# A decoder layer on one core: q and k rotated in fewer operations, one more pair of `up` and two more tiles of the last `dn` group by seven half products

## The chip, the cores and the metric

The kernel runs on one core of a Trainium2 chip. The core has five engines with a queue of instructions each: TensorE (PE in the profile; its weight loads are shown apart as PEld), VectorE (DVE), ScalarE (ACT), GpSimd (POOL), which here only sets memory and issues accumulating DMAs, and SyncE (SP), which issues loads and stores. They meet through semaphores. Times are device microseconds of one execution; the metric is the median of several executions.

## The reference

One decoder layer over 512 tokens of width 1024, in fp32. Cut to what matters:

```python
h = rms_norm(x, mix_norm_g)
u, q, kv, nsa_g, merge_g = split(h @ w_in)
y_pool = pooling_mixer(u, pool_w, pool_scale) @ w_pool_out
y_nsa  = nsa_mixer(q, kv..., gates) @ w_nsa_out      # q, k: rms_norm, then partial_rope; three branches
x = x + (gate_pool * y_pool + gate_nsa * y_nsa) @ w_out
h = rms_norm(x, ffn_norm_g)
gate_pre, val = split(h @ w_up)                      # 2 x 2816 columns
x = x + (silu(causal_dwconv(gate_pre, conv_w, conv_b)) * val) @ w_down

def partial_rope(x, pos):                            # the first 16 of 64 columns of a head
    x1, x2 = x[..., :8], x[..., 8:16]
    return concat([x1 * cos - x2 * sin, x2 * cos + x1 * sin, x[..., 16:]])
```

## The kernel before

**Arithmetic.** Matrices are multiplied in a reduced form of fp32, with each operand split into a high and a low part. A product of one 128x128 block of weights is then three matmuls: high by high, high by low, low by high. The splits are made by ScalarE (the high part is a rounding copy) and VectorE (the low part is a subtraction), or, in `split_by_dma`, by ScalarE and an accumulating DMA that POOL issues, with no VectorE work.

**Stages.** `first` and `round_a` project q and two of the k slots for all tokens, in PSUM banks held over eight rounds. A second group of projections gives the values and gates. Then two streams of PE work run side by side: "m", the attention (rotation, transposes, scores, softmax, averages), and "f", the projections of pooling and merge gates. Then come the output projections (`wno`, `wout`), then the gated MLP: 22 pairs `f` of a gate tile and a value tile of `w_up`, and `w_down` in four groups `dn` of four pairs each, whose work is put between the pairs as `fill`, and a last group `dz` over the pairs 16 to 21, which also adds the residual and stores the result.

**Rotation.** For each of the four tiles of 128 tokens, `rotate(t)` weights and rotates the 16 leading columns of 8 q heads and 4 k heads. The q tile is first multiplied by its norm weights (`gq`); then `rope_on` makes two half products with the sine (one for each half), one with the cosine and one sum. All of it is VectorE work on the tiles `qp`, `kp` and `rt`. The result is transposed by PE (`qk_transpose`). The tables `rope` are computed earlier.

**A pair in plain form** (`up_plain`): the weights of 128 output columns come in one load of 512 KB per half, and 24 matmuls of 512 token columns make the gate, 24 the value.

**A pair in half products** (`up_fast`): gate and value tile are taken as a 2x2 block problem (two halves of the depth, two halves of the tokens) and computed with seven products of half size in place of eight, each of 12 matmuls of 256 columns. For this `half_weights` forms sums of weight quarters on VectorE (`s3`, `r1`, `rg`), and splits seven weight operands: two of them as one tile of 1,024 columns, one of 512 by ScalarE and VectorE (`sh`, `sl`), four of 512 by accumulating DMA. The moving operands (`th`, `tl`) are sums of halves of x, made once in `sums`. Two of the seven products of a pair (`end1`, `end2`) are held and issued in the next pair. Before, pairs 0 and 2 are plain (`PLAIN`), all others in half products.

**The last group** has eight tiles. `dz_plain` makes a tile with 18 matmuls of 512 columns; `dz_fast` makes two tiles with seven half products of 9 matmuls of 256. Their moving operands are `yh`, `yl` and the sums `yth`, `ytl`, made in `y_sums` from y of two pairs three apart. Before, tiles 0 and 1 are plain, and 2 to 7 go in three calls of `dz_fast`.

**What sets the order.** All calls go to a planner (`Plan`), which records them with their dependences and prices and, with a list scheduler, makes one fixed order for each engine. PE's order inside a stream is that of the program; the two streams of the first part are interleaved by the planner, and the other engines' orders are its choice by due times. Tiles come from pools (54 pages of 128x512, rings of three for the raw, high and low weights), and a step whose tile isn't free waits. In `half_weights` the loads of the second weights (`r1`, `r2`) wait for an earlier product, named through the list `begun`.

Of the kernel before, what the change touches and what calls it, by code (L numbers as in the profile page):

```python
# [15 lines left out]
P = 128  # L16
T = 512
NT = 4
# [3 lines left out]
DH = 64  # L22
# [27 lines left out]
NCST = _o  # L50
PAGES = 54
RINGS = {"wraw": 3, "whi": 3, "wlo": 3}
PLAIN = (0,2)
DIRECT = (0,)
AT = (5, 9, 13, 17)
FILL = {f: (0, 0, 0, 0) for f in range(22)}
# [341 lines left out]
def hybrid_layer(ctx: ExitStack, tc: tile.TileContext, xT, xa, pos, par, cst, poolw, w1, wa, wb, wf,  # L398
# [3 lines left out]
    PE, ACT, DVE, POOL, SP = pl.engines  # L402
# [8 lines left out]
    def page(name, shape=(P, T), dt=F32):  # L411
        return pl.tile(sb, shape, dt, name, "pg", PAGES)
# [6 lines left out]
    def keep(name, shape, dt=F32, bufs=1):  # L419
        return pl.tile(sb, shape, dt, name, "t_" + name, bufs)  # L420
# [174 lines left out]
    rope = keep("rope", (P, 2, 5, 2, 8))  # L595
    gq = keep("gq", (P, DH))[:, 0:16]
# [22 lines left out]
    DVE.tensor_copy(rope[:, 0, :, 1], rope[:, 0, :, 0])  # L619
    DVE.tensor_scalar_mul(rope[:, 1, :, 0], rope[:, 1, :, 1], -1.0)  # L620
    DVE.tensor_scalar_mul(gq, ng[:, 0, 0:16], -0.125)
    DVE.tensor_copy(gkv[:, :, 0:16], ng[:, 1:4, 0:16])
    DVE.scalar_tensor_tensor(gkv[:, :, 16:DH], ng[:, 0:1, 16:DH].to_broadcast([P, 3, DH - 16]), -0.125, ng[:, 1:4, 16:DH], op0=ALU.mult, op1=ALU.mult)

# [45 lines left out]
    DVE.tensor_mul(vg, gates[:, :, 0::3].rearrange("p t h -> p h t"),  # L670
                   C("valid")[:, None, :].to_broadcast([P, H, NT]))

    def rope_on(x, tmp, idx, n):
        np_ = x.shape[0]
        ct = rope[:np_, 0, idx].rearrange("p a b -> p (a b)")
        for o, i in ((0, 1), (1, 0)):
            DVE.tensor_mul(tmp[:, :, o * 8:(o + 1) * 8], x[:, :, i * 8:(i + 1) * 8],
                           rope[:np_, 1, idx, o][:, None, :].to_broadcast([np_, n, 8]))
        DVE.tensor_mul(x[:, :, 0:16], x[:, :, 0:16], ct[:, None, :].to_broadcast([np_, n, 16]))
        DVE.tensor_add(x[:, :, 0:16], x[:, :, 0:16], tmp)  # L680

    def rotate(t):
        x, y = qp[t], kp[t]
        DVE.tensor_mul(x[:, :, 0:16], x[:, :, 0:16], gq[:, None, :].to_broadcast([P, 8, 16]))
        y4 = y.rearrange("p (b g) d -> p b g d", b=2)
        DVE.tensor_mul(y4, y4, gkv[:, 1:3][:, :, None, :].to_broadcast([P, 2, 2, DH]))
        tmp = page("rt", (P, 12, 16))
        rope_on(x, tmp[:, 0:8], t, 8)
        rope_on(y, tmp[:, 8:12], t, 4)

    for t in range(NT):
        x, y = qp[t], kp[t]
# [12 lines left out]
    def qk_transpose(t):  # L705
# [7 lines left out]
        if t % 2:  # L713
# [6 lines left out]
            for g in range(2):  # L720
# [4 lines left out]
                ACT.activation(y[r], f32(x[o]), AF.Copy)  # L725

    rotate(0)
    rotate(1)
    turned, flipped = [], []
    for t in range(NT):  # L730
        qk_transpose(t)
        turned.append(pl.last())
        if t + 2 < NT:
            with pl.behind(turned[t]):
                rotate(t + 2)
# [137 lines left out]
    x = keep("kcx", (64, 1, DH))  # L873
# [5 lines left out]
    DVE.tensor_scalar(sm[:, 1:2], sm[:, 0:1], 1.0 / DH, EPS, op0=ALU.mult, op1=ALU.add)  # L879
    rsqrt(sm[:, 2:3], sm[:, 1:2], sm[:, 3:4])  # L880
    DVE.scalar_tensor_tensor(x[:, 0], x[:, 0], sm[:, 2:3], gkv[0:64, 0], op0=ALU.mult, op1=ALU.mult)
    rope_on(x, keep("kct", (64, 1, 24))[:, :, :16], 4, 1)
    ks = keep("kcsp", (64, 2, 2, DH), F32R)
    kx = x.to_broadcast([64, 2, DH])
    split(ks[:, 0], ks[:, 1], kx)
# [5 lines left out]
    ct = keep("cst", (P, 3, T), F32R)  # L891
# [184 lines left out]
    turn = [0]  # L1076
# [6 lines left out]
    for c in range(4):  # L1083
        wh, wl = weights(wno[c].rearrange("p a k n -> p (a k n)"), 1024, "v")
        for f in (2 * c, 2 * c + 1):
            o = (f % 2) * 512
# [104 lines left out]
    def up_plain(f):  # L1191
        pts = []
        for s in range(2):
            wh, wl = weights(flat(wup[f, s]), 1024, "v" if f in DIRECT else "d")
            pt = any_bank()
            if f == 0 and s == 1:
                mm3(pt, wh, wl, gh, gl, 0, 5, nk=KD)
                bcast_rstd(rstd2, rb, "tr")
            mm3(pt, wh, wl, gh, gl, 5 if f == 0 and s == 1 else 0, KD)
            pts.append(pt)  # L1200
            if s == 0:
                begun.append(pl.last())
            if f == 0 and s == 0:
                norm_rstd(acc, rstd2, bank("sc", (P, 2, T))[:, 0])
        pg, pv = pts
        y, g = page("y"), page("fg")
        DVE.tensor_mul(g, pg, rb)
        t = conv(f, g, g)
        DVE.tensor_mul(y, pv, rb)
        DVE.tensor_mul(y, y, t)  # L1210
        split_y(f, y)
# [28 lines left out]
    def fill(n, free=False):  # L1240
        for _ in range(n):
            if fills:
                fills.pop(0)(free)
# [100 lines left out]
    for f in range(KF):  # L1344
        if f in AT:
            dn_group(AT.index(f))
        fill(FILL[f][0], True)
        if f in PLAIN:
            up_plain(f)
# [12 lines left out]
    def dz_plain(f):  # L1362
        wh, wl = weights(flat(wdz[f]), 768, "v")
        pt = any_bank()
        o = page("o")
        mm3(pt, wh, wl, yh, yl, 16, KF, koff=16, nk=KF, first=16)
        begun.append(pl.last())
        DVE.tensor_add(o, pt, x2[f])
        SP.dma_start(out[f], o)
# [3 lines left out]
    def dz_fast(f, e):  # L1373
        L, Rr = slice(0, H2), slice(H2, T)
        a11, a12, h1, h2, h3, h4, h5 = half_weights(flat(wdz[f]), (flat(wdz[e, :, 0:3]), flat(wdz[e, :, 3:6])), 384,
                                                    DZ, begun[-4])
        bx, by, bq = any_bank(), any_bank(), any_bank()
        of, oe = page("o"), page("o")
        product(bx, a11, ymov(0, 0), True, 3)
        begun.append(pl.last())  # L1380
        ACT.activation(by[:, L], bx[:, L], AF.Copy)
        product(bq, h1, ymov(2, 0), True, 3)
        DVE.tensor_sub(oe[:, Rr], x2[e][:, Rr], bq[:, L])
        product(by, h2, ymov(2, 1), False, 3)
        DVE.tensor_add(of[:, Rr], by[:, L], x2[f][:, Rr])
        product(bx, a12, ymov(1, 0), False, 3)
        DVE.tensor_add(of[:, L], bx[:, L], x2[f][:, L])
        SP.dma_start(out[f, :, L], of[:, L])
        product(by, h3, ymov(3, 0), False, 3)
        DVE.tensor_sub(oe[:, Rr], oe[:, Rr], by[:, L])  # L1390
        SP.dma_start(out[e, :, Rr], oe[:, Rr])
        product(bq, h4, ymov(1, 1), False, 3)
        DVE.tensor_add(of[:, Rr], of[:, Rr], bq[:, L])
        SP.dma_start(out[f, :, Rr], of[:, Rr])
        product(by, h5, ymov(3, 1), False, 3)
        DVE.tensor_sub(oe[:, L], x2[e][:, L], by[:, L])
        SP.dma_start(out[e, :, L], oe[:, L])

    for f in range(2):
        dz_plain(f)  # L1400
    for f in range(2, 8, 2):
        dz_fast(f, f + 1)

    pl.emit(TRIES, RESERVE)
# [94 lines left out]
```

## Time and profile before

| | us |
|---|---|
| median of 3 runs | 688.55 (687.68 to 693.29) |
| profiled execution | 687.27 |
| its span, first to last instruction | 685.5 |
| TensorE busy in the span | 680.7 (99%) |
| VectorE busy | 518.8 (76%) |
| ScalarE busy | 443.4 (65%) |

The clock granted to TensorE was 1.00. Matmuls are pipelined and their ends are modelled, so a busy TensorE says only that matmuls follow each other; how fast is read from their starts. All operations are recorded by one helper, so every row has its line, L394, and groups are told apart by tiles: `out<-in` names what an operation writes and reads, without buffer numbers. In a row of groups stand the count, then busy us, mean ns of one, and the idle time of the engine just before, with what ended it. PSUM banks are named `mm`, `tr`, `av` and `sc`.

### The profile page before, as it was taken

To read this page: it belongs to the slowest core of one execution; us is meant where nothing else is said; L and a number is where in the kernel's file an instruction comes from. 1 tells how busy PE (TensorE), PEld (TensorE's weight loads), DVE (VectorE), ACT (ScalarE), POOL (GpSimd) and SP (SyncE) were. 2 spreads that over 40 slices of the span, in tenths; PEclk is the share of its full clock that TensorE was granted. 3 is DMA by queue.
4 is the path that set the end of the run, shared out by engine and by line. 5 is a ranking of instruction groups with operands and counts; after the bars stand their busy time and mean duration, and the time that the engine had idled before them with its cause. 6 is when DMAs were issued, how large, how long until landed. Compare 5 with 4: busy or idle time off the path is not lost.

```text
span 685.5 us, 11622 instructions
## 1 busy us (share of the span) xinstructions
PE 680.7 (99%) x4187; PEld 607.8 (89%) x4187; DVE 518.8 (76%) x1138; ACT 443.4 (65%) x811; POOL 108.0 (16%) x135
## 2 busy tenths in 40 slices
PE   9999999999999999999999999999999999999998
PEld 8898888888888888888888999999999999999898
DVE  6768788888887744777777887777778877688984
ACT  7666477776776654346678876565667657567552
POOL 0010210111111110000122232222223122222121
PEclk9999999999999999999999999999999999999999
DMA  8576644535645557745778989687758766866454
GB/s 303 175 185 203 166 100 116 140 89 145 166 116 151 146 142 239 281 139 172 204 162 197 238 181 217 161 191 172 180 127 205 180 155 168 186 150 154 116 135 106
DMA packets 48585, 115.80 MB, mean 169 GB/s; under 512 B 5520, under 2 KB 9360, under 8 KB 48528
## 3 DMA queue, kind: packets, MB, share of 16 engines
q1 hardware_dynamic: 30960, 76.44, 34.0%
q0 software_dynamic: 17424, 38.48, 31.6%
q8 instruction: 33, 0.54, 0.3%
q14 instruction: 24, 0.20, 0.1%
q10 hardware_dynamic: 144, 0.14, 0.1%
HBM read 70.28 MB, written 6.29 MB: 112 GB/s over the span
## 4 chain that ended last, share of the span: by engine, by line
PE 97%; DMA 1%; DVE 1%; ACT 0%; issue 0%; POOL 0%; POOLq 0%
PE mm L394 37%; PE tr L394 34%; PE sc L394 14%; PE av L394 12%; DMA w<-w 1%; ACT kt L394 0%; DVE qp L394 0%; DVE qt L394 0%; ACT wlo L394 0%; DVE u L394 0%; DVE kt L394 0%; DVE o L394 0%; DVE rt L394 0%; POOL ones L394 0%; POOLq L1490 0%
## 5 line engine op out<-in xcount | busy, mean ns | idle before, releaser
L394 ACT ACTIVATE whi<-wraw 128x1024 fp32r<-128x1024 f32 (+2 forms) x91 | 92.7, 1019 | 41.8 <-PE mm L394 16.1
L394 DVE TENSOR_TENSOR wlo<-wraw,whi 128x1024 fp32r<-128x1024 f32 (+1 forms) x63 | 73.3, 1165 | 5.8 <-ACT whi L394 4.1
L394 PE MATMUL mm<-xh,whi 128*128 128x512 f32 x176 | 72.4, 412 | 0.1
L394 PE MATMUL tr<-tl,sh 128*128 128x256 f32 x250 | 70.1, 280 | 0.0
L394 PE MATMUL mm<-xh,wlo 128*128 128x512 f32 x176 | 69.0, 392 | 0.0
L394 PE MATMUL mm<-xl,whi 128*128 128x512 f32 x176 | 68.9, 391 | 0.0
L394 PE MATMUL tr<-th,sl 128*128 128x256 f32 x240 | 67.7, 282 | 0.0
L394 PE MATMUL tr<-th,sh 128*128 128x256 f32 x240 | 67.7, 282 | 0.0
L394 POOL DMA_DIRECT2D sl<-r x43 | 37.1, 862 | 161.9 <-ACT sl L394 90.8
L394 POOL DMA_DIRECT2D wlo<-wraw x28 | 24.3, 868 | 238.4 <-ACT wlo L394 204.9
L394 PE MATMUL mm<-gh,whi 128*128 128x256 f32 (+1 forms) x320 | 60.8, 287 | 0.0
L394 PEld LDWEIGHTS mm<-gh,whi 128*128 128x128 f32 x320 | 49.5, 188 | 0.6
L394 PEld LDWEIGHTS tr<-tl,sh 128*128 128x128 f32 x250 | 47.2, 189 | 0.5
L394 PEld LDWEIGHTS tr<-th,sh 128*128 128x128 f32 x240 | 45.1, 188 | 1.1
L394 PE MATMUL mm<-gh,wlo 128*128 128x256 f32 (+1 forms) x160 | 45.9, 287 | 0.0
L394 PEld LDWEIGHTS tr<-th,sl 128*128 128x128 f32 x240 | 45.1, 188 | 0.0
L394 DVE SCALAR_TENSOR_TENSOR ft<-fg,pr,ft 128x511 f32<-128x511 f32 (+1 forms) x44 | 32.9, 749 | 12.9 <-ACT ft L394 12.2
L394 PE MATMUL sc<-yh,whi 128*128 128x512 f32 x108 | 42.2, 390 | 0.0
L394 PE MATMUL sc<-yl,whi 128*128 128x512 f32 x108 | 42.0, 389 | 0.0
L394 PE MATMUL sc<-yh,wlo 128*128 128x512 f32 x108 | 42.0, 389 | 0.0
L394 ACT ACTIVATE wlo<-wraw 128x1024 fp32r<-128x1024 f32 x28 | 29.7, 1060 | 15.9 <-PE mm L394 12.9
L394 PEld LDWEIGHTS mm<-xh,wlo 128*128 128x128 f32 x176 | 33.0, 188 | 7.4
(422 smaller groups left out, 1994.1 us busy)
## 6 DMA issues: line engine op xcount, KB each, us to landing
wlo<-wraw POOLq DMA_DIRECT2D x28, 512.0 KB, 4.5
wraw<-wup SPq DMA_DIRECT2D x24, 512.0 KB, 4.2
wraw<-wf SPq DMA_DIRECT2D x22, 512.0 KB, 3.5
r<-wup SPq DMA_DIRECT2D x40, 256.0 KB, 4.3
sl<-r POOLq DMA_DIRECT2D x40, 256.0 KB, 5.0
wraw<-wdn SPq DMA_DIRECT2D x16, 512.0 KB, 3.6
sl<-s POOLq DMA_DIRECT2D x20, 256.0 KB, 5.3
sl<-wraw POOLq DMA_DIRECT2D x20, 256.0 KB, 4.3
```

Of the source, the lines that this page charges most:

```text
L394: getattr(self.real[o.eng], method)(*a, **kw)
```

## The change

The sine and cosine tables for q are multiplied once by the norm weights (`ropeq`, three operations), so that a q tile needs no weighting of its own. The two half products with the sine become one, which reads the halves in turned order through a backward step. A rotation of q is then three operations, a rotation of k three and its weighting. Pair 2 of `up` leaves `PLAIN`, and all eight tiles of the last group go by `dz_fast`. The list `begun` gets one entry for each pair of tiles, so the loads of the last group wait for other products than before. The planner makes its order anew for the whole program.

```diff
-PLAIN = (0,2)
+PLAIN = (0,)
...
+    ropeq = keep("ropeq", (P, 2, NT, 2, 8))
+    gq2 = gq.rearrange("p (a b) -> p a b", a=2)
+    DVE.tensor_mul(ropeq[:, 0], rope[:, 0, 0:NT], gq2[:, None].to_broadcast([P, NT, 2, 8]))
+    for o in range(2):
+        DVE.tensor_mul(ropeq[:, 1, :, o], rope[:, 1, 0:NT, o], gq2[:, None, 1 - o].to_broadcast([P, NT, 8]))
...
-    def rope_on(x, tmp, idx, n):
+    def rope_on(x, tmp, table, n):
         np_ = x.shape[0]
-        ct = rope[:np_, 0, idx].rearrange("p a b -> p (a b)")
-        for o, i in ((0, 1), (1, 0)):
-            DVE.tensor_mul(tmp[:, :, o * 8:(o + 1) * 8], x[:, :, i * 8:(i + 1) * 8],
-                           rope[:np_, 1, idx, o][:, None, :].to_broadcast([np_, n, 8]))
-        DVE.tensor_mul(x[:, :, 0:16], x[:, :, 0:16], ct[:, None, :].to_broadcast([np_, n, 16]))
-        DVE.tensor_add(x[:, :, 0:16], x[:, :, 0:16], tmp)
+        cos, sin = (table[i][:np_, None].to_broadcast([np_, n, 2, 8]) for i in range(2))
+        turn = bass.AP(tensor=x.tensor, offset=x.offset + 8, ap=[list(x.ap[0]), [DH, n], [-8, 2], [1, 8]])
+        x4, tmp4 = (q[:, :, 0:16].rearrange("p n (a b) -> p n a b", a=2) for q in (x, tmp))
+        DVE.tensor_mul(tmp4, turn, sin)
+        DVE.tensor_mul(x4, x4, cos)
+        DVE.tensor_add(x[:, :, 0:16], x[:, :, 0:16], tmp[:, :, 0:16])

     def rotate(t):
         x, y = qp[t], kp[t]
-        DVE.tensor_mul(x[:, :, 0:16], x[:, :, 0:16], gq[:, None, :].to_broadcast([P, 8, 16]))
         y4 = y.rearrange("p (b g) d -> p b g d", b=2)
         DVE.tensor_mul(y4, y4, gkv[:, 1:3][:, :, None, :].to_broadcast([P, 2, 2, DH]))
         tmp = page("rt", (P, 12, 16))
-        rope_on(x, tmp[:, 0:8], t, 8)
-        rope_on(y, tmp[:, 8:12], t, 4)
+        rope_on(x, tmp[:, 0:8], [ropeq[:, i, t] for i in range(2)], 8)
+        rope_on(y, tmp[:, 8:12], [rope[:, i, t] for i in range(2)], 4)
...
-    rope_on(x, keep("kct", (64, 1, 24))[:, :, :16], 4, 1)
+    rope_on(x, keep("kct", (64, 1, 24))[:, :, :16], [rope[:, i, 4] for i in range(2)], 1)
...
-    for f in range(2):
+    for f in range(0):
         dz_plain(f)
-    for f in range(2, 8, 2):
+    for f in range(0, 8, 2):
         dz_fast(f, f + 1)
```

## The prediction

> **What bounds the kernel now.** I read the page's busy times first, then the chain that ended last.
>
> ```profile
> PE 680.7 (99%) x4187; PEld 607.8 (89%) x4187; DVE 518.8 (76%) x1138; ACT 443.4 (65%) x811; POOL 108.0 (16%) x135
> ...
> PE 97%; DMA 1%; DVE 1%; ACT 0%; issue 0%; POOL 0%; POOLq 0%
> ```
>
> PE is busy 99% of the span and is 97% of the chain. A busy PE can still be a slow one, so the next question is whether it waits. The view of waits, PE alone, has two rows:
>
> ```profile
> PE mm L394 <- POOL ones L394: 1.0, 1, 1.0
> PE tr L394 <- DVE qp L394: 0.6, 1, 0.6
> ```
>
> So beyond the start this view has one wait of PE, for VectorE's rotated q. Time can go only by giving PE less to do, or by that one wait. What a matmul costs is read from the chain in order of time (start, us, what, count), where PE runs without a break:
>
> ```profile
> 337.04 5.44 PE tr L394 x24
> ...
> 367.76 5.44 PE av L394 x24
> ...
> 373.20 1.42 PE mm L394 x12
> ...
> 655.97 4.08 PE mm L394 x18
> ...
> 669.63 3.19 PE tr L394 x27
> ```
>
> The first row is the last tile of `wout`: 24 matmuls of 512 columns take 5.44 us, 0.227 each, and a half product of 12 matmuls of 256 columns takes 1.42, 0.118 each: half the columns cost 52% of the time, not 50%. The row at 367.76 is the value half of pair 2 itself, the row at 655.97 is tile 1 of the last group (18 matmuls), and the row at 669.63 is three half products of tiles that already run in the new form (9 matmuls, 1.063 each).
>
> What the other engines have left is read by stage (PE, PEld, DVE, ACT, POOL, clock, DMA share, GB/s):
>
> ```profile
> 348.50:361.90 13.40, 13.40 (x92) 12.39 (x93) 6.92 (x22) 9.46 (x15) 3.48 (x4) 1.00 0.90 198
> 361.90:372.80 10.90, 10.90 (x51) 9.08 (x50) 9.78 (x15) 8.94 (x16) 3.45 (x4) 1.00 0.87 222
> 372.80:382.70 9.90, 9.90 (x84) 9.84 (x83) 8.72 (x15) 8.23 (x15) 3.30 (x4) 1.00 0.79 181
> 382.70:392.70 10.00, 10.00 (x87) 10.00 (x86) 8.98 (x17) 8.23 (x15) 2.74 (x4) 1.00 1.00 244
> ...
> 635.00:651.50 16.50, 16.50 (x87) 14.20 (x86) 15.38 (x28) 8.29 (x15) 1.72 (x2) 1.00 0.43 113
> 651.50:659.60 8.10, 8.10 (x37) 6.73 (x36) 7.48 (x14) 6.33 (x12) 2.61 (x3) 1.00 0.25 49
> 659.60:682.00 22.40, 22.40 (x189) 22.32 (x189) 13.87 (x30) 6.53 (x15) 3.49 (x4) 1.00 0.61 150
> ```
>
> The second row is pair 2, the third and fourth are pairs 3 and 4. The clock is 1.00 throughout. VectorE is the tight neighbour (8.98 of 10.00), and in pair 4 the DMA engines are full (1.00). The last three rows are the end of `up` with the last of the group's fills, the two plain tiles, and the six tiles already in half products.
>
> **Pair 2.** PE loses 2 x 24 matmuls of 512, 2 x 5.44 = 10.88, and gains seven half products, 7 x 1.42 = 9.94: **0.94 us less**, all of it on the path. [...]
>
> VectorE gets the work of recombining the weights. Rows of VectorE and ScalarE in 348 to 400:
>
> ```profile
> L394 DVE TENSOR_TENSOR wlo<-wraw,whi 128x1024 fp32r<-128x1024 f32 x5 | 6.1, 1218 | 0.0
> L394 DVE TENSOR_TENSOR wraw<-wraw 128x512 f32<-128x512 f32 x5 | 3.4, 685 | 0.0
> ...
> L394 DVE TENSOR_TENSOR y<-y,rb 128x256 f32<-128x256 f32 x3 | 1.3, 419 | 0.0
> ...
> L394 ACT ACTIVATE whi<-wraw 128x1024 fp32r<-128x1024 f32 x7 | 7.4, 1053 | 0.6 <-PE av L394 0.5
> L394 ACT ACTIVATE sl<-r 128x512 fp32r<-128x512 f32 x7 | 4.4, 624 | 0.0
> ...
> L394 ACT ACTIVATE u<-tr 128x256 f32<-128x256 f32 x6 | 2.3, 382 | 2.4 <-PE tr L394 1.8 <-ACT sh L394 0.6
> ```
>
> Added are one low part of 1,024 columns (1.22), four sums and one low part of 512 (5 x 0.685) and six output steps of 256 (6 x 0.42): 7.2 us. Two full-width output steps (2 x 0.69, as at 353.83 below) go. Net **+5.8 us of VectorE**. ScalarE loses four copies of 1,024 and gets one of 1,024, nine of 512 and three of 256: 9 x 0.62 + 3 x 0.38 - 3 x 1.05 = +3.6 us, and it has 44.2 - 34.9 = 9.3 free in the first four stages above. POOL issues four accumulating DMAs of 256 KB in place of two of 512 KB, and SP three loads in place of two; the bytes are the same. On SP the two new loads wait for the end of the last `wout` tile, 337.04 + 5.44 = 342.5, and pair 3's load is queued behind them; both are asked for well after 350. I cost all this at nothing because of two covers. The first is idle time just ahead:
>
> ```profile
> 353.83 0.69 DVE L394 TENSOR_TENSOR fg<-av,rb 128x512 f32<-128x512 f32 x1 [0.64 <-ACT rb L394]
> 355.26 0.69 DVE L394 TENSOR_TENSOR y<-mm,rb 128x512 f32<-128x512 f32 x1 [0.73 <-PE mm L394]
> 358.31 1.53 DVE L394 SCALAR_TENSOR_TENSOR ft<-fg,pr,ft 128x511 f32<-128x511 f32 x2 [2.35 <-ACT ft L394]
> 361.93 0.69 DVE L394 TENSOR_TENSOR y<-y,ft 128x512 f32<-128x512 f32 x1 [2.09 <-ACT ft L394]
> ```
>
> The brackets are idle time of VectorE: 0.64 + 0.73 + 2.35 + 2.09 = 5.8 us in the ten ahead of pair 2, where the changed kernel's order places pair 2's low part and four sums (4 of the 7.2 us). The second is how early the weights of the next pairs are. The latest is pair 4's first accumulated one: issued on POOL at 377.94, read by PE at 388.88, with a median of 7.0 from issue to landing in this stage.
>
> ```profile
> 377.94 0.86 POOL L394 DMA_DIRECT2D sl<-r  x1 [0.18 <-ACT u L394]
> ...
> 388.88 0.28 PE L394 MATMUL av<-th,sl 128*128 128x256 f32 x1
> ...
> sl<-r POOLq DMA_DIRECT2D x8, 256.0 KB, 7.0
> ```
>
> That is 10.94 - 7.0 = 3.9 us to spare, of which PE's own gain takes 0.94. No new wait of PE is planned by the code; if both covers go, the price is in the first rival below.
>
> **Tiles 0 and 1 of the last group.** PE loses 2 x 4.08 = 8.16 and gets seven half products of 1.063, 7.44: **0.72 us less**. VectorE loses two low parts and two sums over 512 columns, and gets one low part, six steps of 384 and six of 256:
>
> ```profile
> L394 DVE TENSOR_TENSOR wlo<-wraw,whi 128x768 fp32r<-128x768 f32 x5 | 4.8, 954 | 0.5 <-ACT whi L394 0.4
> L394 DVE TENSOR_TENSOR wraw<-wraw,r 128x384 f32<-128x384 f32 x3 | 1.7, 559 | 0.1
> ```
>
> 0.95 + 6 x 0.56 + 6 x 0.42 - 2 x 0.95 - 2 x 0.69 = **+3.5 us**. From 635 to 682 it has 47.0 - 15.38 - 7.48 - 13.87 = 10.3 us free. One dependence is new: a plain tile reads the last y in its last block, while the second half product reads sums of all six. The last y ends VectorE's part here:
>
> ```profile
> 645.20 0.69 DVE L394 SCALAR_TENSOR_TENSOR y<-y,ft 128x512 f32<-128x512 f32 x1 [0.16 <-ACT ft L394]
> 645.81 0.76 DVE L394 SCALAR_TENSOR_TENSOR ta<-ta,y 128x256 f32<-128x256 f32 x2
> ```
>
> The sum is formed by 646.6; a copy and a low part of some 0.7 each bring it to about 648. PE asks for it at 651.5 + 1.06, so it is covered by 4 us, and I take nothing for it; without that cover all later products would queue behind it on PE.
>
> **The rotation.** PE's one wait in order of time, the operations of its chain by tile, and an idle time of VectorE further ahead:
>
> ```profile
> 66.55 0.39 PE L394 MATMUL mm<-xh,wlo 128*128 128x512 f32 x1
> 67.56 0.41 PE L394 MATMUL tr<-cs,qp 128*128 128x128 f32 x2 [0.61 <-DVE qp L394]
> ...
> L394 DVE TENSOR_TENSOR rt<-qp,rope x8: 217/221/226, 50.9 to 66.5; 128x64 f32<-128x64 f32 x8
> L394 DVE TENSOR_TENSOR rt<-kp,rope x8: 182/183/193, 55.9 to 69.1; 128x32 f32<-128x32 f32 x8
> L394 DVE TENSOR_TENSOR qp<-qp,rt x4: 284/293/294, 52.7 to 67.1; 128x128 f32<-128x128 f32 x4
> ...
> 40.04 1.28 DVE L394 TENSOR_REDUCE small<-qp 128x8 f32<-128x512 f32 x2 [3.90 <-ACT qp L394]
> ```
>
> From start to start the step is 1.01 in place of 0.227: 0.78 us lost. A q tile now takes five operations: the weighting (0.29), two half-rotations (0.22 each), the cosine and the sum. It takes three after: 0.29 + 0.44 - 0.29 = 0.44 less. The first operation reads with a backward step, which the trace does not show; its ends are the 0.29 of the same 128 elements and the two it replaces, 0.44, and I take 0.29. A k tile saves 2 x 0.18 - 0.22 = 0.15. Ahead of the awaited fourth q tile that is 4 x 0.44 + 2 x 0.15 = 2.1 us. The three table operations are paid in the 3.9 us of idle time before 40.04. But the order changes: the fourth tile's transposes now stand behind 36 feature matmuls and not 42, and PE asks 6 x 0.227 = 1.4 us sooner. 2.1 - 1.4 = 0.7 of the 0.78 would go; the bounds are 0 and 0.78, and I take **0.5 us**, since the same reordering puts the second tile's transposes directly behind the first's.
>
> **The sum.** 0.94 + 0.72 + 0.5 = 2.2 us. The profiled execution took 687.27 (span 685.5 and 1.8 around it), so 685.1; from the median of the runs shown, 688.55, it would be 686.4. The profiled one lies below even the lowest run shown, 687.68, so I put the forecast between: **685.8 us**.
>
> **The rivals.**
> *VectorE and the DMA engines behind it become the bound in pairs 2 to 4 (slower).* Pairs 1 to 4 would now follow each other in half products. For: 8.98 of 10.00 busy, DMA share 1.00 in pair 4. Against: the 5.8 us of idle time. If none of it serves, weights come 5.8 us later against a spare of 3.9; the stage then ends 1.9 us later than now, whatever PE saves in it. It decides from a delay of 3.9 us on. With the tail's 0.72 and nothing from the rotation: 687.27 + 1.9 - 0.7 = 688.5, and 689.8 on the median's base. If pair 5 slips by as much again with nothing to spare, 5.8 more come on top: 694.3, and 695.6 on the median's base.
> *The reordered first 260 us wait elsewhere.* The planner interleaves anew there; the waits that PE has are 0.6 and 1.0 long, so I price one more at 1.0 and the rotation's gain as lost. 687.27 - 1.66 + 1.0 = 686.6. The other way, small waits vanish too: 684.
> *The half products are no shorter: the change doesn't do what it says.* Each matmul has its weight load:
>
> ```profile
> L394 PEld LDWEIGHTS tr<-th,sh 128*128 128x128 f32 x240 | 45.1, 188 | 1.1
> ```
>
> If a 188 ns load did not hide, a half matmul would cost 0.118 + 0.188 = 0.306, and the 84 and 63 of them 45.0 in place of 19.0 us: 713 in all. The 1.42 us rows of the same products elsewhere show that it hides. [...]
>
> **Chances.** Forecast 0.62; VectorE or DMA late 0.18, a third of it beyond one per cent; first stage anew and slower 0.13, or better 0.06; half products no shorter 0.01. One per cent, 6.9 us, is about what a measurement here can tell from no change, and the forecast is a third of it. Faster by over 1% needs 681.7, below all terms together (684.8): 0.02. Slower by over 1%: 0.06 + 0.01 = 0.07. Within: 0.91. The range runs from 683.6 (all of the rotation, and some small waits) to 690.0 (the slower rival on the median's base).
>
> **What will show it.** In the chain after, pair 2 as runs of 12 at 1.42, and about 28 half products of 9 at 1.06 at the end; from the first `up` matmul to the last matmul 1.7 us less; PE's view of waits without the row for qp. Wrong would be: a PE wait on `sl`, `sh` or `yl` between 360 and 400, on `ytl` or `sl` after 650, or a new one between 50 and 260; or 128x256 matmuls that no longer follow at 0.118.

## The result and the profile after

The changed kernel takes 695.16 us (median of 7 runs, 691.69 to 695.93) against 687.77 for the kernel before (7 runs): a ratio of 1.0085, 95% interval 1.0063 to 1.0107. It was forecast to be 2 us faster and is some 4 to 7 us slower. The profiled execution took 695.16, its span is 693.4 (685.5 before).

The page, busy times and chain:

```profile
PE 681.8 (98%) x4250; PEld 609.2 (88%) x4250; DVE 523.9 (76%) x1147; ACT 448.9 (65%) x828; POOL 112.3 (16%) x140
...
PE 79%; DMA 10%; issue 4%; DVE 3%; ACT 2%; POOL 0%; SPq 0%; POOLq 0%; ACTq 0%; DVEq 0%
```

The engines' shares have hardly moved, but PE has fallen from 97% of the chain to 79%, and 10% is now DMA. So the loss is not work but waiting. The view of waits, PE alone (releaser: us in total, times, longest):

```profile
PE tr L394 <- ACT u L394: 3.7, 4, 1.5
PE mm L394 <- DMA sl<-r: 1.3, 1, 1.3
PE mm L394 <- POOL ones L394: 1.0, 1, 1.0
PE sc L394 <- DVE yl L394: 0.8, 1, 0.8
PE tr L394 <- DVE qp L394: 0.5, 1, 0.5
PE sc L394 <- ACT yh L394: 0.3, 1, 0.3
PE tr L394 <- DVE sl L394: 0.2, 1, 0.2
```

Before, two of these rows were there. Where the time goes is seen when every matmul's step to the next is compared with its undisturbed duration (0.227 us for 512 columns, 0.117 for 256, and what the other shapes mostly take) and the excess is summed by stretch. Worked out from the traces, in us; the first stretch holds the loads at the start, which differ from profile to profile (2.3 to 4.1 in this table and in that of the experiments):

```
                  0-40  40-260  260-360  360-420  420-620  620-end    sum
before             3.6     4.0      0.0      0.4      1.4      0.4    9.9
after              2.9     5.0      0.0      5.5      4.4      1.6   19.4
```

The excess has grown by 9.5 us. The half products save 0.94 + 0.72 = 1.66, and 9.5 - 1.66 = 7.8 is, but for 0.1, the growth of the span. It has two large parts: 5.1 us between 360 and 420, in pairs 2 to 6 of `up`, and 3.0 us between 420 and 620, in the pairs behind them.

The stages of the prediction again, after (PE, PEld, DVE, ACT, POOL, clock, DMA share, GB/s):

```profile
348.50:361.90 13.40, 13.40 (x92) 12.39 (x93) 10.78 (x28) 9.25 (x18) 4.30 (x5) 1.00 0.54 98
361.90:372.80 10.90, 10.90 (x95) 10.90 (x94) 8.95 (x17) 10.18 (x19) 3.44 (x4) 1.00 0.86 186
372.80:382.70 9.90, 8.61 (x73) 8.41 (x72) 8.23 (x15) 7.43 (x15) 3.44 (x4) 1.00 0.90 186
```

VectorE did move its new work into the idle time ahead (6.92 to 10.78 in the first row) and is no fuller than before in the other two. What changed in the first row is the DMA share: 0.54 where it was 0.90. From 348 to 358 it is 0.45 (0.83 before), and then PE waits 1.3 us for weights.

The chain in order of time (start, us, what) shows how that goes on, from pair 2 to PE's wait at 413:

```profile
359.24 7.63 DMA r<-wup
...
373.37 6.12 DMA sl<-wraw
...
382.04 7.16 DMA r<-wup
...
402.22 4.93 DMA sl<-wraw
...
407.29 5.10 DMA wraw<-wup
...
413.44 0.37 ACT u L394
...
413.86 1.69 PE tr L394 x12
```

Until the last row PE is not in this stretch of the chain. It is a ring: second weights are loaded (`r<-wup`), recombined, and their low parts accumulated by DMA; when the last accumulating DMA of a pair (`sl<-wraw`) has landed, the pair's ring slot is free and a later pair's first weights (`wraw<-wup`) may be loaded; and behind that load on SP stand the next second weights. SP's timeline after:

```profile
339.62 0.33 SPq L394 DMA_DIRECT2D wraw<-wup  x1
340.07 0.83 SPq L394 DMA_DIRECT2D r<-wup  x2
358.31 0.33 SPq L394 DMA_DIRECT2D wraw<-wup  x1
358.73 0.98 SPq L394 DMA_DIRECT2D r<-wup  x2
369.13 0.33 SPq L394 DMA_DIRECT2D wraw<-wup  x1
369.51 2.22 SPq L394 DMA_DIRECT2D r<-wup  x2
```

The rows are the first load of pair 3, the second loads of pair 2, the first load of pair 4, the second loads of pair 3, the first load of pair 5, the second loads of pair 4. SP stands still from 340.9 to 358.3; its waits between 339 and 371 are

```profile
SPq L394 <- DMA sl<-wraw: 26.5, 2, 17.3
```

17.3 us for pair 1's last accumulating DMA, which landed at 358.15 (issued at 354.85, 3.3 us to landing). The load that waited for it went at 358.31, and pair 3's second loads, next on the queue, 0.42 us later, at 358.73: in this trace they move only when the load ahead of them has. In the kernel before the same loads are these:

```profile
354.65 1.65 SPq L394 DMA_DIRECT2D r<-wup  x2
360.80 3.36 SPq L394 DMA_DIRECT2D wraw<-wup  x2
364.22 0.90 SPq L394 DMA_DIRECT2D r<-wup  x2
```

Pair 3's second loads go at 354.65 and pair 4's at 364.22: 4.1 and 5.3 us sooner. There SP's long wait, just ahead of 354, is for another kind of DMA:

```profile
SPq L394 <- DMA wlo<-wraw: 16.6, 2, 14.1
```

`wlo<-wraw` is the accumulating DMA of pair 2 in the plain form, which frees its slot as soon as the low part of the raw weights is made. Pair 3's first load took that slot, and pair 3's second loads stood behind nothing that waited for pair 1.

### The profile page after: what moved, and what is told of

Its sections match the earlier page's. It is cut to its first block, busy times and chain, and to the rows that moved or that the text cites. A ratio compares the mean times of both kernels' runs of the same rounds, so it can differ in the third digit from the quotient of the medians.

```text
span 693.4 us, 11819 instructions
## 1 busy us (share of the span) xinstructions
PE 681.8 (98%) x4250; PEld 609.2 (88%) x4250; DVE 523.9 (76%) x1147; ACT 448.9 (65%) x828; POOL 112.3 (16%) x140
## 4 chain that ended last, share of the span: by engine, by line
PE 79%; DMA 10%; issue 4%; DVE 3%; ACT 2%; POOL 0%; SPq 0%; POOLq 0%; ACTq 0%; DVEq 0%
PE mm L394 33%; PE tr L394 25%; PE av L394 11%; PE sc L394 11%; DMA r<-wup 6%; DMA sl<-r 2%; DMA sl<-wraw 2%; DMA wraw<-wup 1%; ACT sh L394 1%; DVE ft L394 1%; DMA x<-xa 0%; ACT whi L394 0%; ACT sl L394 0%; POOL sl L394 0%; DVE fg L394 0%
## 5 line engine op out<-in xcount | busy, mean ns | idle before, releaser
L394 POOL DMA_DIRECT2D sl<-r x46 | 39.6, 860 | 155.0 <-ACT sl L394 70.8
L394 PE MATMUL tr<-gh,whi 128*128 128x256 f32 x336 | 61.5, 281 | 0.0
L394 PEld LDWEIGHTS tr<-gh,whi 128*128 128x128 f32 x336 | 51.5, 188 | 0.1
L394 PE MATMUL tr<-gh,wlo 128*128 128x256 f32 x168 | 47.3, 282 | 0.0
L394 ACT ACTIVATE sl<-r 128x512 fp32r<-128x512 f32 (+1 forms) x46 | 28.2, 613 | 19.4 <-DMA r<-wup 14.7
L394 ACT ACTIVATE pp<-pp,asm 128x384 f32<-128x384 f32 (+3 forms) x64 | 35.3, 556 | 5.2 <-DVE asm L394 5.2
L394 PEld LDWEIGHTS mm<-xh,whi 128*128 128x128 f32 x176 | 33.1, 188 | 6.4 <-DVE u L394 1.6
L394 PEld LDWEIGHTS mm<-xl,whi 128*128 128x128 f32 x176 | 33.2, 189 | 4.5
L394 PE MATMUL tr<-th,sh 128*128 128x256 f32 x110 | 31.5, 286 | 3.8 <-ACT u L394 3.7
L394 POOL DMA_DIRECT2D sl<-wraw x25 | 21.5, 860 | 78.2 <-ACT sl L394 63.8
```

The costliest lines, as they stand in the source:

```text
L394: getattr(self.real[o.eng], method)(*a, **kw)
```

## The experiments

Theory A: the second loads are late, because they queue on SP behind a load that waits for a ring slot. Rival B: VectorE's 5.8 us more. Rival C: any new order of the planner gains or loses some microseconds. Rival D: the rotation or the tiles 0 and 1.

**Pair 2 alone, and all but pair 2.**

```diff
 # pair2_alone: the kernel before with
-PLAIN = (0,2)
+PLAIN = (0,)
 # no_pair2: the changed kernel with
-PLAIN = (0,)
+PLAIN = (0,2)
```

> Pair 2 in half products, the rotation and the last group's tiles 0 and 1 as in the kernel before. Theory A (second loads late: pair 2 in the new form holds its ring slots until its last accumulating DMA has landed, so that the first load of pair 4 waits for a slot until about 358 and the second loads of pair 3, behind it on SP, with it) and rival B (VectorE's 5.8 us more in pairs 2 to 4) both expect the loss to be here: the 5.0 us lost between 360 and 420 less the 0.94 gained give 691.8; with the four later stalls (3.7 us) as well, 695.5. Rival D (the rotation or the tiles 0 and 1 made the loss) expects 686.8, the gain alone. Under A the second loads of pair 3 are issued after 357 and PE waits for sl near 378; under B PE's weights are late although the loads are not.

> The changed kernel with pair 2 in the plain form again: the new rotation and tiles 0 and 1 in half products remain. A and B expect the loss gone and the two small gains left: 687.8 - 0.7 - 0.15 (what the rotation returned in the profile after) = 686.9, and no PE wait between 340 and 620. D expects 694 or more. If only the late stalls at 475, 537 and 600 stay, 690.5: then those belong to the new order of the whole plan and not to pair 2 (rival C).

Measured: pair 2 alone 692.44 against 688.12, ratio 1.0065 (1.0048 to 1.0082); without pair 2 688.66, ratio 1.0012 (1.0001 to 1.0024). D falls: the loss comes with pair 2. Without it PE waits nowhere between 340 and 620, but the two small gains are not there either. With pair 2 alone the second loads of pairs 3 and 4 are as late as A said (358.11 and 368.61), behind a load that waits for a slot (pair 1's, though the expectation reads as if it were pair 2's), and PE waits 0.8 us for `sl` near 378. But only 1.2 us are lost between 360 and 420, where A had expected 5.0, and 4.0 us in the later stalls (both in the table of excess further below). That 692.44 lies near A's 691.8 is luck. The same late loads cost a different amount in another order.

**The second loads first.** The planner gets one more rule of order for SP: a pair's second loads are emitted ahead of the next pair's first load. The rule sets order alone; the loads wait for nothing new.

```diff
 # r_first: the changed kernel with, in half_weights,
         SP.dma_start(rg[:, :2 * w], first)
+        if last_r and w == 512:
+            pl.turns.append((last_r[0], pl.last()))
...
             SP.dma_start(r2[:, :w], second[1])
+        last_r[:] = [pl.last()]
 # and in Plan.run and Plan.dues: of each pair in turns, the second is picked only after the first has started
```

> The changed kernel in whole, with one more rule of order for the planner: on SP the second loads of a pair stand ahead of the first load of the pair behind it, so that they do not queue behind a load that waits for a ring slot. VectorE's work is the same. A expects the second loads of pair 3 to be issued before 350, no wait of PE for sl or yl between 360 and 420, and 5 us back: 690 if the late stalls stay, 686 if they go with it. B expects no change, 694 to 696, with the loads early and VectorE late all the same.

Measured: 688.30 against 688.12, ratio 1.0005 (0.9990 to 1.0020): the loss is gone. SP's timeline of this kernel:

```profile
344.24 2.99 SPq L407 DMA_DIRECT2D r<-wup  x2
359.10 0.33 SPq L407 DMA_DIRECT2D wraw<-wup  x1
363.35 3.01 SPq L407 DMA_DIRECT2D r<-wup  x2
```

Pair 4's first load goes no sooner (359.10), but pair 3's second loads went at 344.24. This also moves traffic ahead (DMA share 0.99 from 340 to 348, 0.84 in the changed kernel). DMA issues between 356 and 376, with the median time to landing, first of the changed kernel and then of this one:

```profile
sl<-r POOLq DMA_DIRECT2D x4, 256.0 KB, 7.5
...
r<-wup SPq DMA_DIRECT2D x4, 256.0 KB, 7.4
```

```profile
sl<-r POOLq DMA_DIRECT2D x4, 256.0 KB, 4.4
...
r<-wup SPq DMA_DIRECT2D x2, 256.0 KB, 3.2
```

The late loads were thus also slow ones here, 7.4 us in place of 3.2; those of pair 3, issued at 358.73, ran beside accumulating DMAs of pair 2 that were issued at 357.37, 358.62 and 359.66. And here the landing is what became shorter: the accumulating DMA of pair 3 that PE waits for in the changed kernel was issued at 370.94 there and took 8.7 us to land (median of its kind 7.5); with the rule it was issued later, at 372.41, and the median was 4.4. VectorE's work is the same, so B is hard to hold. The rule makes a new order, too: of the excess, 5.0 us are gone between 360 and 420 and 2.9 behind 420, where the order alone also changes the stalls.

**A fourth ring slot, and what its room cost.**

```diff
 # ring4: the changed kernel with
-PAGES = 54
-RINGS = {"wraw": 3, "whi": 3, "wlo": 3}
+PAGES = 52
+RINGS = {"wraw": 4, "whi": 3, "wlo": 3}
 # pages52: the changed kernel with PAGES = 52 alone
```

> The changed kernel with four ring slots for the raw weights in place of three, and 52 pages in place of 54 to make room. A expects the first load of pair 4 not to wait for pair 1's slot any more, the second loads of pair 3 to go at least 8 us sooner than 358, and 686 to 690, the price of two pages unknown. B expects 694 to 696.

> The changed kernel with 52 pages in place of 54 and three ring slots as it has: what the two pages alone cost, since the run with four slots paid for them. If the pages made its 10 us, 703 to 706, with the same stall of some 3 us near 200; if the fourth slot itself did, 693 to 696, and the second loads were not early with it for a reason of its own.

Measured: 705.57, ratio 1.0254 (1.0232 to 1.0276), and 707.96 with the two pages taken away alone, 1.0270 (1.0235 to 1.0305). So the pages made the loss (2 us more than the 703 to 706 expected, with some 3 us lost near 200 in both), and a slot more returned nothing that could be told from zero. A part of it is PE's clock: the mean granted was 0.995 and 0.993 in the profiled executions, an estimated 3.5 and 5 us of these spans (0.005 x 703 and 0.007 x 708). A's own expectation failed here too: the second loads of pair 3 did not come sooner. SP's timeline with four slots says why:

```profile
361.81 0.33 SPq L394 DMA_DIRECT2D wraw<-wup  x1
362.23 1.23 SPq L394 DMA_DIRECT2D r<-wup  x2
```

The second row is pair 3's second loads, the first row the first load of pair 5: the planner used the slot to ask for one more pair ahead, and that load waits for pair 1's slot as pair 4's did. What decides is the place in the queue, not the number of slots.

**VectorE relieved, the order kept.**

```diff
 # dve_less: the changed kernel, planned as it is; these are not emitted for pairs 1 to 5
-        DVE.scalar_tensor_tensor(t[:, 1:], g[:, :T - 1], ...)
-        DVE.scalar_tensor_tensor(t[:, 2:], g[:, :T - 2], ...)
-        DVE.tensor_mul(y[:, H2:], y[:, H2:], rb[:, H2:])
-            DVE.tensor_mul(g[:, H2:], g[:, H2:], rb[:, H2:])
```

> The changed kernel in its own order, with 20 of VectorE's operations left out: the convolution's two taps and the scaling by rb of the second half of y and of g, in pairs 1 to 5. That is 2.3 us of VectorE in each pair (2 x 0.75 + 2 x 0.42), 7 us in pairs 2 to 4, more than the 5.8 that pair 2 added; nothing on SP and no DMA is touched. B (VectorE) expects PE's waits between 360 and 420 gone: 688 to 690. A (second loads late) expects the first load of pair 4 at about 358 and the second loads of pairs 3 and 4 at about 358 and 369 as before it, and the wait of PE for sl near 378 still there: 692 to 695.

Measured: 695.36 against 688.36, ratio 1.0100 (1.0072 to 1.0128): no faster. The stages, and PE's wait:

```profile
372.80:382.70 9.90, 9.70 (x82) 9.49 (x81) 6.60 (x11) 7.64 (x15) 3.20 (x4) 1.00 0.94 193
382.70:392.70 10.00, 7.77 (x65) 7.57 (x65) 7.22 (x12) 8.69 (x18) 2.83 (x4) 1.00 0.94 211
```

```profile
PE mm L398 <- DMA sl<-r: 2.4, 2, 2.2
```

VectorE is at 6.60 of 9.90 and 7.22 of 10.00, and PE waits longer for the accumulated weights than it did (2.4 us in place of 1.3). PE's waits for `yh`, `yl` and `u` between 360 and 420, 2.6 us in the changed kernel, are not there, so VectorE had a hand in those; but the time did not come back. An estimated 1.7 us of this execution (0.38 x 4.5, last section) are a slower PE clock, but the other three, at clock 1.00, took 692.90 to 696.96. B falls as the cause of the loss.

**Another order.** The planner makes twelve orders and emits the one it rates best; here the fifth is emitted in place of the fourth.

```diff
 # after_try4
-            if best is None or spans < best[0]:
+            if i == 4:
```

> The changed kernel with another of the planner's tries emitted (the fifth in place of the fourth); its order on SP is the same up to pair 7. If the loss is chance of one order (rival C), it should come out anywhere between 686 and 695 and lie at other places. A expects the first stretch to be the same, 3 to 5 us lost between 360 and 420 with the second loads of pair 3 at about 358, and only the late stalls of ScalarE's copy u to move: 690 to 695.

Measured: 690.48 against 688.36, ratio 1.0032 (1.0018 to 1.0045). The excess between 360 and 420 is 3.9 us (5.5 in the changed kernel), with the second loads of pair 3 again behind the long wait:

```profile
359.03 0.33 SPq L394 DMA_DIRECT2D wraw<-wup  x1
359.47 0.85 SPq L394 DMA_DIRECT2D r<-wup  x2
```

Between 420 and 620 it is 1.4, as in the kernel before. So the first part of the loss came again with another order, though 1.6 us smaller, and the later stalls did not: C is right for those.

**One place alone.** The rule for pair 4's first load only.

```diff
 # turn_3: r_first with
-        if last_r and w == 512:
+        if len(rs) in (3,) and w == 512:        # rs: one entry per half_weights so far
```

> The changed kernel with the rule of order for one place only: on SP the second loads of pair 3 stand ahead of the first load of pair 4; pair 4's still stand behind pair 5's first load, which waits for pair 2's slot. If the whole loss is the inheritance of that one late load, its cure is enough: 686 to 690, no PE wait before 420. If every pair's second loads are late by the slot that the load ahead of them waits for, the wait at 378 (pair 4's) stays: pair 3's go before 350, pair 4's still at 366 to 369, and 690 to 694.

Measured: 692.87 against 689.22, ratio 1.0065 (1.0040 to 1.0090); the profiled run is the lowest of its ten, 690.6. PE's waits:

```profile
PE av L408 <- ACT u L408: 1.7, 1, 1.7
...
PE tr L408 <- ACT u L408: 0.9, 2, 0.5
```

The excess between 360 and 420 is 0.7: the one swap cured that stretch, and PE's wait at 378 is gone. That wait was for pair 3's weights, not pair 4's as the expectation has it (the rows stand under "the second cover" below). Pair 4's second loads went at 366.48 in place of 369.51, so they had inherited some of their lateness. The time, however, came out in the range of the other answer, because the later stalls are all there (4.8 us between 420 and 620).

**The small parts, and the rule without pair 2.**

```diff
 # rot_alone: the changed kernel with PLAIN = (0,2) and dz_plain for f in range(2)
 # dz_alone: the kernel before with dz_fast for f in range(0, 8, 2) and no dz_plain
 # r_first_norot: pair 2, tiles 0 and 1 and the rule of r_first, with the rotation as before
 # r_first_before: the kernel before with the rule of r_first
```

> The new rotation alone; pair 2 and tiles 0 and 1 as in the kernel before. The prediction's term (0.5 us saved at PE's one wait) gives 687.6. The profile of the kernel without pair 2 speaks for the rival that the reordered first 260 us wait elsewhere: there the wait for qp is still 0.5, and 0.37, 0.42 and 0.37 us appear in 80-100, 140-160 and 180-200, against 0.18 less in 60-80: 688.1 + 1.0 = 689.1, and these three places show again with the rotation alone.

> Tiles 0 and 1 of the last group in half products alone. The prediction's term gives 688.1 - 0.72 = 687.4, with the qp wait and the first 260 us as in the kernel before. If the tail gives back what it gains (in the kernel without pair 2 about 0.8 us of small extra gaps lie between 620 and 680), 688.1, and the gaps are there again.

> Pair 2 and tiles 0 and 1 in half products, the old rotation, and the rule of order that sets the second loads ahead of the next pair's first load. With the loads early the forecast's terms for PE (0.94 + 0.72) should be there: 686.5; 685.8 if the wait for qp is gone as in the kernel with pair 2 alone; 687.3 if one late stall of ScalarE's copy u stays as in the kernel with the rule and the new rotation. If the rule had helped by chance of the order only, nothing holds it here: 688 to 693.

> The kernel before with the same rule of order and nothing else. Theory A: its loads are early enough already (no wait of PE for weights), so the rule can return nothing: 687.5 to 688.7. If the rule is worth its 7 us by itself, whatever pair 2 does, 681.

All against 688.22. The rotation alone: 688.91, ratio 1.0006 (0.9995 to 1.0016). Tiles 0 and 1 alone: 688.07, 1.0001 (0.9990 to 1.0012). The rule on the kernel before: 688.32, 1.0003 (0.9989 to 1.0016), so it is worth nothing where no load is late. Pair 2 and the tiles with the rule and the old rotation: **686.46, ratio 0.9977 (0.9967 to 0.9987)**, faster than both kernels. The excess in all of them (us):

```
                  0-40  40-260  260-360  360-420  420-620  620-end    sum
pair2_alone        4.1     3.2      0.0      1.6      5.4      0.4   14.7
no_pair2           3.7     4.5      0.1      0.4      1.4      1.2   11.3
r_first            3.6     5.0      0.0      0.5      2.5      0.6   12.4
turn_3             2.4     5.0      0.0      0.7      4.8      1.5   14.4
after_try4         3.5     4.9      0.0      3.9      1.4      1.5   15.3
rot_alone          3.1     5.0      0.0      0.4      1.4      1.5   11.4
dz_alone           2.3     3.5      0.0      0.4      1.4      1.9    9.6
r_first_norot      3.3     3.2      0.0      0.5      2.2      1.0   10.1
r_first_before     3.1     3.2      0.0      0.4      4.4      0.5   11.7
```

**What the runs show together.** With pair 3's second loads issued at 358 to 359.5, behind the long wait, the stretch from 360 to 420 lost 1.2 us (pair 2 alone), 3.5 (the other order) and 5.1 us (the changed kernel) more than in the kernel before; with them ahead of it, at 342 to 346, 0.1 to 0.3 in three orders (with the rule, with the rule and the old rotation, with the rule at one place). So the queue on SP is shown as the cause there; how much it costs depends on the rest of the order.

**What stays open.** The stalls between 420 and 620 (0 to 4 us above the 1.4 of before) come and go with the order, with pair 2 in the new form or without. Their chain in the changed kernel also runs through second loads:

```profile
581.95 6.53 DMA sl<-r
...
589.02 6.73 DMA r<-wup
...
597.53 0.95 ACT whi L394
```

An accumulating DMA of one pair ends, the next pair's second load follows it, and ScalarE's copies stand behind that. Which trait of an order brings them was not settled, and no run here changes them alone.

## Why the prediction was wrong, and where it was right

**What bounds the kernel.** That PE's waits decide was right. That only two existed said nothing of how near the next was.

**Pair 2, PE's term.** Right. In the chain of the version with the rule and the old rotation, pair 2's products stand as forecast (two of 12 matmuls, 0.118 each):

```profile
365.36 2.83 PE mm L407 x24
```

With the loads early the time is 0.23% of 688.2 shorter, 1.6 us (0.9 to 2.3), which is the size of 0.94 + 0.72. It shows the two terms together and not each: in its trace 0.8 us less is lost between 40 and 260, and 1.4 more behind 420.

**Pair 2, the first cover.** Right: VectorE's idle time took the new work, and relieving VectorE returned nothing.

**Pair 2, the second cover.** This is the step that failed: "10.94 - 7.0 = 3.9 us to spare". The spare was counted for pair 4 from the issue of its accumulating DMA, as if that issue had a fixed place. It follows the pair's second loads, and these went 5.3 us later for pair 4 (364.22 to 369.51) and 4.1 us later for pair 3 (354.65 to 358.73). PE met pair 3's first. The awaited accumulating DMA of pair 3, and the matmul that reads what it made, after:

```profile
370.94 0.86 POOL L394 DMA_DIRECT2D sl<-r  x1 [0.18 <-issue]
```

```profile
379.67 0.39 PE L394 MATMUL mm<-th,sl 128*128 128x256 f32 x1 [1.29 <-DMA sl<-r]
```

It landed at 379.62. In the kernel before it was issued at 366.72, landed at 373.91 and was read at 378.95. Its spare of 5.0 us was used up by 4.2 us of later issue, 1.5 us of longer landing (8.7 in place of 7.2) and 0.7 us by which PE came sooner; 1.4 us were missing. So the 7.0 was too short here as well. Pair 4's DMA landed at 389.52, 0.2 us before PE read it, and that only because PE had lost the 1.4 already.

A sentence ahead of it named the queue and followed it two loads too short: "pair 3's load is queued behind them; both are asked for well after 350". Behind pair 3's first load and pair 2's second ones stands pair 4's first, that one waits for pair 1's slot until 358.3, and pair 3's second loads are behind it. A moved step's loads were counted; which load now waits for which slot, and what is queued behind that, was not.

The same passage took the gate of the second loads for a wait. It orders the plan only: on the chip pair 2's second loads went at 340.07, behind pair 3's first load (339.62) and before the last tile of `wout` had ended (342.5).

**Tiles 0 and 1.** The products take what was said, as in this row of the chain after:

```profile
671.79 3.19 PE tr L394 x27
```

No wait for `ytl` came; that cover held. But the 0.72 us do not show in the time: alone it is 1.0001, and in its trace 1.5 us more are lost behind 620, of which 0.6 is one wait for VectorE's `sl`. The rotation alone, with these tiles plain, loses 1.1 us more there too, so such losses can come with the order and need not come from the tiles.

**The rotation.** The backward-reading operation was priced well: 0.29 forecast, and the tile's rows show

```profile
L394 DVE TENSOR_TENSOR rt<-qp,ropeq x4: 281/284/292, 50.3 to 62.8; 128x128 f32<-128x128 f32 x4
```

The wait did not go, since the new order asks for the tile sooner:

```profile
63.89 0.63 PE L394 MATMUL tr<-cs,qp 128*128 128x128 f32 x4 [0.46 <-DVE qp L394]
```

That is 3.7 us ahead of 67.56, of which the loads at the start give 0.7 (2.9 against 3.6 in the table); the count of matmuls had given 1.4. And 0.4 us more was lost at each of three places between 80 and 200. The same wait is gone in three kernels with the old rotation whose order differs (pair 2 alone, and the two with the rule and the old rotation). Here PE's waits in one of them:

```profile
PE mm L407 <- POOL ones L407: 1.0, 1, 1.0
PE av L407 <- ACT u L407: 0.5, 1, 0.5
```

The wait went with the order in these three; it stayed, at 0.5 us, in each kernel with the shorter rotation.

**The rivals.** The first rival's worst case, 694.3 to 695.6, is what came, with a chance of 0.06. Its place (pairs 2 to 5) and its wait (on `sl`) were right, its cause (VectorE) was not. That its number is the measured one is luck: 3.0 of the 7.8 us lie in later stalls, of which it said nothing. The second, the first 260 us anew, was right in kind and size: 1.0 us more between 40 and 260. The range ended at the milder case of the first rival, because its condition was read from VectorE's idle time, which held. One per cent was taken for what a measurement can tell from no change; the intervals here reach 0.1 to 0.4% to each side, and the loss of 0.85% is clear of them.

## What to carry to other kernels

When a step is changed that holds ring slots or buffers, write down the order of the loads on the issuing queue, and beside each load which slot it needs and what frees it; a load that may go is late if the one ahead of it may not, as pair 3's second loads were here (358.73, and 344.24 with nothing ahead that waited for pair 1's slot). A pair or tile in a simpler form can be the one that lets the loads run ahead, and its own time does not show that. Where a planner orders everything anew, small gains of less than 1 us are to be tried in more than one of its orders, since here the order alone moved 0 to 4 us.

## What the runs showed of the hardware

PE's granted clock fell after two of the three waits of 2.1 to 2.6 us that are shown here. The columns are as in the stages above; first the kernel with VectorE relieved, after a wait of 2.2 us, then the one with four slots, after one of 2.1, then pair 2 alone, after one of 2.6:

```profile
392.00:396.50 4.50, 4.50 (x26) 4.50 (x27) 1.93 (x3) 2.33 (x5) 1.03 (x2) 0.62 1.03 202
```

```profile
449.50:453.50 4.00, 4.00 (x19) 3.44 (x18) 3.96 (x8) 0.94 (x3) 0.48 (x1) 0.64 0.97 284
```

```profile
442.50:446.00 3.50, 3.05 (x19) 2.81 (x20) 3.47 (x7) 3.30 (x8) 1.29 (x2) 1.00 0.78 204
```

After the waits of 2.2 and 2.1 us the clock was 0.62 and 0.64, after the one of 2.6 it was 1.00. With four slots it was 0.96 from 453.5 to 460.0 as well, so the fall cost an estimated 1.7 us there (0.36 x 4.0 + 0.04 x 6.5). In the run with 52 pages PE was busy for 1.15 of the 5.0 us from 466 to 471, and the clock was 0.91 in these and 0.50 from 471.0 to 476.4. The length of the wait alone thus does not tell when the clock fell; what does was not settled. In the changed kernel, with waits of 1.5 us at most, the clock stays at 1.00.
